# Gathers that convert on the way in, and rests between them

## The chip, the cores and the metric

The kernel runs on one core of one Trainium2 chip. The core has a matrix engine (TensorE, PE), a vector engine (VectorE, DVE), a scalar engine (ScalarE, ACT), a general engine (GpSimd, POOL) and a sync engine (SyncE, SP) that issues transfers. Sixteen DMA engines move data between the chip's main memory and the core's own memory. The metric is the device time of one launch in microseconds (us). Before the change it was 438.41 us, the median of three runs (437.76 to 445.43).

## The reference

```python
B, S, N, D = (16, 4096, 2048, 512)
gathered = x[b_idx, indices, :].copy()      # x float32 [B, S, D]; indices sorted, int64 [B, N]
cs = np.cumsum(gathered, axis=1)            # running sum over the N gathered rows of each batch
return np.matmul(cs, w).astype(np.float32)  # w float32 [D, D]; result [B, N, D]
```

For each of 16 batches, 2048 rows of 512 numbers are picked out of 4096, summed up as they come, and each running sum is multiplied by one 512 by 512 matrix. 67 MB are gathered and 67 MB are written.

## The kernel before

The 16 x 2048 output rows are cut into T = 256 tiles of 128 rows, and each two tiles form a group (R = 2). One batch is NT = 16 tiles. A tile goes through six steps, each on an engine of its own:

- `gather` (line 129, Pool): an indirect DMA fetches the tile's 128 rows of x, 256 KB, into a float32 slot `g32`. There are NG = 16 tile slots. A gather into a used slot first waits until the cast of the tile that was there is done (semaphore `s_c`).
- `cast` (line 150, ScalarE): copies the slot to float16 in `g16` (16 tiles as well). `casts` (lines 116 to 124) is a list worked out beforehand of which tiles are cast at which step: up to FAR = 6 tiles ahead, mostly two tiles in one instruction of 1024 columns, and one at a time near both ends.
- `sums` (line 158, PE): four matmuls with a triangular matrix of ones. Each gives, for 128 of the 512 columns, the running sums inside the tile, already transposed, in a PSUM buffer `pa` (NA = 4).
- `carry` (line 175, DVE): adds the last column of the tile before and writes float16 to `cst`. Each carry needs the one before it. At the start of a batch it is a plain copy (line 185).
- `project` (line 202, PE): four matmuls of `cst` with the float16 matrix `w16` into a PSUM buffer `pb` (NB = 4).
- `drain` (line 219, ScalarE): copies `pb` to one of NO = 4 output buffers `ob`, four tiles each.

SyncE stores an output buffer, 1 MB, as soon as its four tiles are drained (`store`, line 224); the first and last two groups are stored in smaller pieces. ScalarE works through its steps strictly in order: at each fourth tile it waits until the output buffer's last store is done (`s_o`), then come the casts of that step, then the drain. PE's order is a list written out beforehand (lines 350 to 358): LEAD = 3 tiles of sums ahead of the projections. Inside the sums and the projections stand waits for the buffer that the next step needs, between the first and second or the second and third matmul. DVE, PE and ScalarE run the middle of the work in hardware loops (`Fori`), 16 tiles a turn; Pool's and SyncE's instructions are written out in full. Ahead of all this the indices are loaded, transposed on PE to one per partition, and written back as integers.

In an ordinary group the tiles' rows are interleaved: partition p of the group's tiles holds neighbouring rows, so that one store descriptor covers two rows. The groups in `PLAIN`, the first two and the last two, are in plain row order, so that each tile can be summed, projected and stored by itself.

Of the kernel before, what the change touches and what calls it, by code (L numbers as in the profile page):

```python
# [7 lines left out]
P = 128  # L8
FP32 = mybir.dt.float32
FP16 = mybir.dt.float16  # L10
# [23 lines left out]
def kernel(  # L34
# [7 lines left out]
    nc = tc.nc  # L42

    B, S, D = x.shape
    N = indices.shape[1]
    R = 2
# [3 lines left out]
    T = B * NT  # L50
    G = T // R
# [1 line left out]
    KI = T // P  # L53
    FIRST = 2 * R
    NG = 16
    LEAD = 3
    FAR = 6
    NH = 8
    NA = 4
    NB = 4  # L60
    NC = 4
    W = 2
    H = 1
    NO = 4
    U = NT
    V = max(U, W * R * NO)
    assert V % U == 0 and V % (W * R * NO) == 0 and T % V == 0 and U % NG == 0 and U % NA == 0 and U % (R * NC) == 0 and U % NB == 0
    assert D == 512 and N % (R * P) == 0 and T % P == 0

    x_flat = x.rearrange("b s d -> (b s) d")  # L70
# [1 line left out]
    const = ctx.enter_context(tc.tile_pool(name="const", bufs=1))  # L72
# [8 lines left out]
    ut = const.tile([P, R, Q], FP16)  # L81
    uq = const.tile([P, P], FP16)
    ident = const.tile([P, P], FP32)
    zeros = const.tile([P, D], FP16)
    spare = const.tile([P, 1], FP16)
    g32 = [const.tile([P, R, D], FP32, name=f"g32_{i}") for i in range(NG // R)]
    g16 = [const.tile([P, R, D], FP16, name=f"g16_{i}") for i in range(NH)]
    cst = [const.tile([P, DC, R, P], FP16, name=f"cst{i}") for i in range(NC)]
    ob = [const.tile([P, W, R, D], FP32, name=f"ob{i}") for i in range(NO)]
    pa = [ps.tile([P, DC, R, Q], FP32, name=f"pa{i}") for i in range(NA)]  # L90
# [11 lines left out]
    s_w = [sem(f"s_w{c}") for c in range(DC)]  # L102
    s_idx = [sem(f"s_idx{k}") for k in range(KI)]
    s_ol = sem("s_ol")
    s_g = [sem(f"s_g{i}") for i in range(NG)]
    s_o = [sem(f"s_o{i}") for i in range(NO)]
    s_a = sem("s_a")
    s_d = sem("s_d")
    s_b = sem("s_b")
    s_e = sem("s_e")  # L110

    pool, pe, dve, act, sp = (
        Lane(e) for e in (nc.gpsimd, nc.tensor, nc.vector, nc.scalar, nc.sync)
    )

    casts = []
    cast_by = []
    for u in range(T):
        far = min(FAR, 2 if u < R else 3 + (u + 4) // 8, 3 + (T - 1 - u) // 6)
        casts.append([])  # L120
        while len(cast_by) <= min(u + far, T - 1):
            n = R if far > 5 and len(cast_by) % R == 0 else 1
            casts[u].append((len(cast_by), n))
            cast_by += [cast_by[-1] + 1 if cast_by else 1] * n

    for u in range(2 * U + U, T - 2 * U):
        assert casts[u] == [(t + U, n) for t, n in casts[u - U]]

    def gather(t):
        g, r = divmod(t, R)  # L130
        if t >= NG:
            pool.need(s_c, cast_by[R * (g + 1) - NG - 1])
        if t < FIRST:
            pool.need(s_first[g], 16)
            ap = idx_first[:, t, 0:1]
        else:
            pool.need(s_prep, t // P + 1)
            ap = idxg[:, t // P, t % P : t % P + 1]
        nc.gpsimd.indirect_dma_start(  # L139
            out=g32[g % (NG // R)][:, r, :],  # L140
            out_offset=None,
            in_=x_flat,
            in_offset=bass.IndirectOffsetOnAxis(ap=ap, axis=0),
            element_offset=(t // NT) * S * D,
        ).then_inc(s_g[t % NG], 16)


    PLAIN = (0, 1, G - 2, G - 1)

    def cast(t, n, first=None):  # L150
        g, r = divmod(t, R)
        for u in range(t, t + n):
            act.need(s_g[u % NG], 16 * (u // NG + 1), first)
        nc.scalar.copy(  # L154
            out=g16[g % NH][:, r : r + n], in_=g32[g % (NG // R)][:, r : r + n]
        ).then_inc(s_c, 1)

    def sums(t, u, first=None):
        g, r = divmod(t, R)
        tiles = None if first is None else R * first  # L160
        pe.need(s_c, cast_by[t] if first is None else cast_by[2 * U + t] - 2 * U // R, first)
        pe.need(s_d, t - NA + 1, tiles)
        for c in range(DC):
            if c == 1 and u is not None:
                pe.need(s_e, u - NB + 1, tiles)
            mm = nc.tensor.matmul(  # L166
                out=pa[t % NA][:, c],
                lhsT=g16[g % NH][:, r, c * P : (c + 1) * P],
                rhs=uq[:] if first is None and g in PLAIN else ut[:],
                start=(c == 0),  # L170
                stop=(c == DC - 1),
            )
        mm.then_inc(s_a, 1)
# [28 lines left out]
    def project(u, t, first=None):  # L202
        g, j = divmod(u, R)
        tiles = None if first is None else R * first
        pe.need(s_e, u - NB + 1, tiles)
        pe.need(s_d, u + 1 if first is None and g in PLAIN else R * (g + 1), tiles)
        for c in range(DC):
            if c == 2 and t is not None:
                pe.need(s_d, t - NA + 1, tiles)
            mm = nc.tensor.matmul(  # L210
                out=pb[u % NB][:],
                lhsT=cst[g % NC][:, c, j, :],
                rhs=w16[:, c, :],
                start=(c == 0),
                stop=(c == DC - 1),
            )
        mm.then_inc(s_b, 1)
# [6 lines left out]
    def store(g, n):  # L224
        b, h = divmod(g, GB)
        rows = out[b, h * R * P : (h + n) * R * P, :]
        src = ob[g // W % NO]
        if g in (0, G - 1):
            for j in range(R):
                sp.need(s_e, R * g + j + 1)  # L230
                nc.sync.dma_start(
                    out=rows[j * P : (j + 1) * P, :], in_=src[:, g % W, j]
                ).then_inc(s_ol if g else (s_o[0], s_of)[j >= H], 16)
            return
        sp.need(s_e, R * (g + n))
        order = "(g j p) d -> p g j d" if g in PLAIN else "(g p j) d -> p g j d"
        rows = rows.rearrange(order, p=P, j=R)
        src = src[:, g % W : g % W + n]
        if n < W:
            done = s_ol if g >= W else (s_o[0], s_of)[R + g > H]  # L240
            nc.sync.dma_start(out=rows, in_=src).then_inc(done, 16)
            return
        for i in range(H):
            part = slice(i * P // H, (i + 1) * P // H)
            nc.sync.dma_start(out=rows[part], in_=src[part]).then_inc(s_o[g // W % NO], 16)
# [23 lines left out]
    for g in range(G - W, G):  # L269
        store(g, 1)  # L270
    for i in range(G // W - NO, G // W - 1):
        sp.need(s_o[i % NO], 16 * H * (i // NO + 1))
    sp.need(s_ol, 16 * (R + W - 1))


# [4 lines left out]
        out=ident[:],  # L280
        in_=ident[:],
# [7 lines left out]
        out=ut[:],  # L289
        in_=ut[:],  # L290
# [9 lines left out]
        out=uq[:],  # L300
        in_=uq[:],
# [5 lines left out]
    ).then_inc(s_ut, 1)  # L307
    for t in range(T):
        gather(t)
    nc.gpsimd.drain()  # L310


# [12 lines left out]
    for k in range(KI):  # L325
# [3 lines left out]
            out=pb[k % NB][:, :P], in_=idxf[:, k, :], identity=ident[:]  # L329
# [29 lines left out]

    head = order.index((False, 2 * U - 1)) + 1  # L360
    tail = order.index((False, T - 2 * U - 1)) + 1
    step = 2 * U
    for i in range(head + step, tail):
        assert order[i] == (order[i - step][0], order[i - step][1] + U)

    def run(i, first=None):
        is_sums, t = order[i]
        after = next((v for k, v in order[i + 1 :] if k != is_sums), None)
        if first is not None:
            t -= 2 * U  # L370
            after -= 2 * U
        if is_sums:
            sums(t, after, first)
        else:
            pe.need(s_wc, DC)
            project(t, after, first)

    for i in range(head):
        run(i)
    with nc.tensor.Fori(2 * U // R, (T - 2 * U) // R, U // R) as first:  # L380
        pe.new_pass()
        for i in range(head, head + step):
            run(i, first)
# [19 lines left out]

    for u in range(2 * U):
        step(u)
    with nc.scalar.Fori(2 * U, T - 2 * U, V) as first:
        act.new_pass()
        for u in range(V):
            step(u, first)
    for u in range(T - 2 * U, T):  # L410
        step(u)
# [30 lines left out]
```

## Time and profile before

| what | value |
|---|---|
| median of three runs | 438.41 us |
| profiled execution | 440.94 us |
| its span, first to last instruction | 439.2 us |
| granted TensorE clock, mean | 0.892 |
| HBM read and written | 68.42 MB, 67.11 MB |
| longest chain: PE, issue, DVE, unknown queue | 74%, 10%, 7%, 7% |

The profile is of one execution. Busy times are given per engine; a group of instructions is one source line with one shape, with its count, its busy time in us, the mean of one in ns, and the idle time ahead of it by what ended it. A row of waits gives the waiting instruction, what it waited for, the total in us, the number of times and the longest. A row of the order in time starts with its start and its duration in us, and ends with the idle time ahead of it. "issue" is idle time without a wait that the profile shows, and "remote" stands for a queue or core that it cannot name. In the row of digits, each digit is the busy share of the DMA engines in one of 40 equal slices, in tenths. In the table by stage, x stands for how many instructions started in it, and PEclk for the granted clock.

### The profile page before, as it was taken

How to read it: one execution, taken by the hardware profiler on the slowest of the kernel's cores; microseconds unless marked ns; L12 is line 12 of the kernel's file. 1: busy time of each engine (PE TensorE's matmuls, PEld its weight loads, DVE VectorE, ACT ScalarE, POOL GpSimd, SP SyncE). 2: the span in 40 equal slices, each digit the busy share in tenths (PEclk: the TensorE clock that was granted, in tenths of full speed). 3: DMA queues.
4: the chain of work that ended last, by engine and by line, in shares of the span. 5: the costliest groups of instructions: out<-in, count | busy, mean ns of one | idle time of the engine just before them, and what ended most of it. 6: DMA issues, size and time to landing. Idle time of an engine off the chain costs nothing.

```text
span 439.2 us, 6408 instructions
## 1 busy us (share of the span) xinstructions
PE 329.8 (75%) x2066; PEld 171.5 (39%) x2066; DVE 178.4 (41%) x263; ACT 263.6 (60%) x407; POOL 243.7 (55%) x266
## 2 busy tenths in 40 slices
PE   6518687777877786679787697768777697876995
PEld 2203343343434343335344353434334343443552
DVE  2104343444344444345344344344345353543552
ACT  4216566556665665576656575566576666665794
POOL 6764557565655566556565465565555665655300
PEclk9756989798989899988899698996989969998898
DMA  7864979799888999989898899988989999999966
GB/s 225 256 212 156 347 273 344 252 336 364 285 318 304 333 351 328 350 294 339 316 353 295 310 336 335 359 318 273 366 310 328 331 337 328 300 330 349 331 242 241
DMA packets 39884, 135.68 MB, mean 309 GB/s; under 512 B 5825, under 2 KB 6081, under 8 KB 39873
## 3 DMA queue, kind: packets, MB, share of 16 engines
q0 software_dynamic: 20480, 67.13, 47.9%
q1 hardware_dynamic: 18832, 67.90, 38.9%
q10 hardware_dynamic: 560, 0.53, 0.4%
q8 instruction: 5, 0.08, 0.1%
q14 instruction: 7, 0.05, 0.0%
HBM read 68.42 MB, written 67.11 MB: 309 GB/s over the span
## 4 chain that ended last, share of the span: by engine, by line
PE 74%; issue 10%; DVE 7%; another core or an unknown queue 7%; ACT 1%; DVEq 0%; ACTq 0%; SPq 0%
PE pb L210 55%; PE pa L166 18%; DVE cst L198 7%; PE pb L316 1%; DVE cst L185 0%; ACT ob L222 0%; ACT g L154 0%; PE pb L328 0%; DVEq L26 0%; DVE zeros L320 0%; DVEq L437 0%; ACTq L26 0%; SPq L93 0%
## 5 line engine op out<-in xcount | busy, mean ns | idle before, releaser
L210 PE MATMUL pb<-w,cst 128*128 128x512 f16 x1024 | 293.1, 414 | 84.7 <-DVE cst L198 60.1
L139 POOL DMA_INDIRECT g<-in_x_dram,idxg x252 | 238.2, 945 | 165.1 <-ACT g L154 97.6
L198 DVE TENSOR_TENSOR cst<-pa,cst 128x512 f16<-128x512 f32 x240 | 166.1, 692 | 231.3 <-PE pa L166 162.2
L222 ACT COPY ob<-pb 128x512 f32<-128x512 f32 x256 | 146.2, 591 | 164.6 <-PE pb L210 108.1
L210 PEld LDWEIGHTS pb<-w,cst 128*128 128x128 f16 x1024 | 94.3, 104 | 164.9 <-DVE cst L198 65.8
L154 ACT CAST g<-g 128x1024 f16<-128x1024 f32 (+1 forms) x147 | 138.4, 945 | 0.3 <-issue 0.2
L166 PE MATMUL pa<-ut,g 128*128 128x128 f16 x992 | 103.9, 230 | 16.0 <-issue 12.8
L166 PEld LDWEIGHTS pa<-ut,g 128*128 128x128 f16 x992 | 81.5, 104 | 87.7 <-issue 33.8
L185 DVE CAST cst<-pa 128x512 f16<-128x512 f32 x16 | 11.0, 686 | 16.2 <-PE pa L166 12.6
L316 PE MATMUL pb<-zeros 128*128 128x512 f16 x16 | 5.9, 538 | 1.5 <-DVE zeros L320 1.5
L139 POOL DMA_INDIRECT g<-in_x_dram,idx_first x4 | 4.0, 994 | 1.6 <-issue 0.9
L166 PE MATMUL pa<-uq,g 128*128 128x128 f16 x32 | 3.1, 219 | 1.9 <-issue 1.8
L166 PEld LDWEIGHTS pa<-uq,g 128*128 128x128 f16 x32 | 2.2, 97 | 4.2 <-issue 3.1
L316 PEld LDWEIGHTS pb<-zeros 128*128 128x128 f16 x16 | 2.1, 135 | 4.2 <-issue 2.2
L392 ACT CAST w<-w 128x512 f16<-128x512 f32 x2 | 1.1, 616 | 3.4 <-DMA w<-in_w_dram 3.4
L389 ACT ACT_TABLE_LOAD x1 | 1.3, 1283 | 2.5 <-issue 2.5
L323 DVE CAST idxf<-idx 128x128 f32<-128x128 uint32 x2 | 0.5, 227 | 3.8 <-DMA idx<-in_indices_dram 3.8
L337 DVE CAST w<-w 128x512 f16<-128x512 f32 x2 | 0.8, 422 | 1.6 <-DMA w<-in_w_dram 1.6
L328 PE MATMUL pb<-ident,idxf 128*128 128x128 f32 x2 | 0.9, 447 | 0.0
L328 PEld LDWEIGHTS pb<-ident,idxf 128*128 128x128 f32 x2 | 0.4, 206 | 0.9 <-issue 0.9
L320 DVE MEMSET zeros<- 128x256 uint32 x1 | 0.3, 272 | 1.1 <-SPq L93 1.1
L334 DVE CAST idxg<-pb 128x128 uint32<-128x128 f32 x2 | 0.6, 292 | 0.3 <-PE pb L328 0.2
(11 smaller groups left out, 2.1 us busy)
## 6 DMA issues: line engine op xcount, KB each, us to landing
out_dram<-ob SPq DMA_DIRECT2D x62, 1024.0 KB
g<-in_x_dram,idxg POOLq DMA_INDIRECT x252
out_dram<-ob SPq DMA_DIRECT2D x4, 256.0 KB, 2.8
out_dram<-ob SPq DMA_DIRECT2D x2, 512.0 KB, 3.4
w<-in_w_dram ACTq DMA_DIRECT2D x2, 256.0 KB, 3.3
w<-in_w_dram SPq DMA_DIRECT2D x2, 256.0 KB
idx<-in_indices_dram SPq DMA_DIRECT2D x2, 128.0 KB, 2.6
g<-in_x_dram,idx_first POOLq DMA_INDIRECT x4
```

The source lines that it names most:

```text
L139: nc.gpsimd.indirect_dma_start(out=g32[g % (NG // R)][:, r, :], out_offset=None, in_=x_flat, in_offset=bass.IndirectOffsetOnAxis(ap=ap, ax ...
L154: nc.scalar.copy(out=g16[g % NH][:, r : r + n], in_=g32[g % (NG // R)][:, r : r + n]).then_inc(s_c, 1)
L166: mm = nc.tensor.matmul(out=pa[t % NA][:, c], lhsT=g16[g % NH][:, r, c * P : (c + 1) * P], rhs=uq[:] if first is None and g in PLAIN else ...
L185: nc.vector.tensor_copy(out=dst, in_=src).then_inc(s_d, 1)
L198: nc.vector.tensor_tensor(out=dst, in0=src, in1=last, op=mybir.AluOpType.add).then_inc(s_d, 1)
L210: mm = nc.tensor.matmul(out=pb[u % NB][:], lhsT=cst[g % NC][:, c, j, :], rhs=w16[:, c, :], start=(c == 0), stop=(c == DC - 1),)
L222: nc.scalar.copy(out=ob[g // W % NO][:, g % W, j], in_=pb[u % NB][:]).then_inc(s_e, 1)
L316: nc.tensor.matmul(out=pb[NB - 1][:], lhsT=zeros[:, :P], rhs=zeros[:], start=True, stop=True)
L328: nc.tensor.transpose(out=pb[k % NB][:, :P], in_=idxf[:, k, :], identity=ident[:]).then_inc(s_pt, 1)
L337: nc.vector.tensor_copy(out=w16[:, c, :], in_=w32[:, c, :]).then_inc(s_wc, 1)
L389: nc.scalar.copy(out=spare[:], in_=zeros[:, :1])
L392: nc.scalar.copy(out=w16[:, c, :], in_=w32[:, c, :]).then_inc(s_wc, 1)
```

## The change

The gather writes float16. Its target is `g16` itself, now the only set of gather slots, 16 tiles; the conversion takes place in the DMA. `g32`, `cast`, `casts` and FAR are gone, so ScalarE only drains. A gather into a used slot waits for PE's sums of the tile that was there (`s_a`), once for each pair of tiles. Sums wait for the gather itself (`s_g`, now 32 semaphores for 16 slots, which suits the longer loop of PE). LEAD is 4. After each four gathers Pool sets one row of 512 float16 numbers per partition of an otherwise unused tile `rest` to zero. PE's loop holds 32 tiles a turn. In its loop the tile numbers are absolute. The stores keep their pieces and their rows; the code that names their semaphores is shorter, and H, which was 1, is gone. The first and last two groups stay in row order.

```diff
     NG = 16
-    LEAD = 3
-    FAR = 6
-    NH = 8
+    NS = 32
+    FREE = 2
+    LEAD = 4
...
     U = NT
-    V = max(U, W * R * NO)
+    V = NS
...
-    g32 = [const.tile([P, R, D], FP32, name=f"g32_{i}") for i in range(NG // R)]
-    g16 = [const.tile([P, R, D], FP16, name=f"g16_{i}") for i in range(NH)]
+    rest = const.tile([P, T // NB, D], FP16)
+    g16 = [const.tile([P, R, D], FP16, name=f"g16_{i}") for i in range(NG // R)]
...
-    s_g = [sem(f"s_g{i}") for i in range(NG)]
+    s_g = [sem(f"s_g{i}") for i in range(NS)]
...
     def gather(t):
         g, r = divmod(t, R)
-        if t >= NG:
-            pool.need(s_c, cast_by[R * (g + 1) - NG - 1])
+        if t % FREE == 0:
+            pool.need(s_a, t + FREE - NG)
...
         nc.gpsimd.indirect_dma_start(
-            out=g32[g % (NG // R)][:, r, :],
+            out=g16[g % (NG // R)][:, r, :],
...
-        ).then_inc(s_g[t % NG], 16)
+        ).then_inc(s_g[t % NS], 16)
...
     def sums(t, u, first=None):
         g, r = divmod(t, R)
         tiles = None if first is None else R * first
-        pe.need(s_c, cast_by[t] if first is None else cast_by[2 * U + t] - 2 * U // R, first)
-        pe.need(s_d, t - NA + 1, tiles)
+        skip = 0 if first is None else 2 * U
+        pe.need(s_g[t % NS], 16 * (t // NS + 1) - skip // R, first)
+        pe.need(s_d, t - NA + 1 - skip, tiles)
...
-                lhsT=g16[g % NH][:, r, c * P : (c + 1) * P],
-                rhs=uq[:] if first is None and g in PLAIN else ut[:],
+                lhsT=g16[g % (NG // R)][:, r, c * P : (c + 1) * P],
+                rhs=uq[:] if g in PLAIN else ut[:],
...
     for t in range(T):
         gather(t)
+        if t % NB == NB - 1:
+            nc.gpsimd.memset(rest[:, t // NB, :], 0.0)
...
-    with nc.tensor.Fori(2 * U // R, (T - 2 * U) // R, U // R) as first:
+    with nc.tensor.Fori(2 * U // R, (T - 2 * U) // R, V // R) as first:
...
     def step(u, first=None):
-        if first is None and u == min(W * R * NO, 2 * U - 1):
-            act.need(s_of, 16 * (R + W - 1 - H))
         if u % (W * R) == 0:
-            stored = first if first is None else first * (16 * H) // (R * W * NO)
-            act.need(s_o[u // R // W % NO], 16 * H * (u // R // W // NO), stored)
-        for t, n in casts[u if first is None else 2 * U + u]:
-            cast(t if first is None else t - 2 * U, n, first)
+            if first is None and u == W * R * NO:
+                act.need(s_of, 16 * (R + W - 2))
+            act.need(s_o[u // R // W % NO], 16 * (u // R // W // NO), first)
         drain(u, first)
```

More of the change, by code (lines that the diff above doesn't have):

```diff
@@ L62 @@
     W = 2
-    H = 1
     NO = 4
     U = NT
-    V = max(U, W * R * NO)
-    assert V % U == 0 and V % (W * R * NO) == 0 and T % V == 0 and U % NG == 0 and U % NA == 0 and U % (R * NC) == 0 and U % NB == 0
+    V = NS
+    assert V % NS == 0 and NS % NG == 0 and FREE == R and NS == 16 * R and 2 * U % NS == 0 and (T - 4 * U) % V == 0 and U % (W * R * NO) == 0 and U % NA == 0 and U % (R * NC) == 0 and U % NB == 0
     assert D == 512 and N % (R * P) == 0 and T % P == 0
@@ L114 @@
     )
[L116 to L127, printed above, removed]
     def gather(t):
         g, r = divmod(t, R)
-        if t >= NG:
-            pool.need(s_c, cast_by[R * (g + 1) - NG - 1])
+        if t % FREE == 0:
+            pool.need(s_a, t + FREE - NG)
         if t < FIRST:
@@ L144, in gather @@
             element_offset=(t // NT) * S * D,
-        ).then_inc(s_g[t % NG], 16)
+        ).then_inc(s_g[t % NS], 16)
     PLAIN = (0, 1, G - 2, G - 1)
[L150 to L156, printed above, removed]
     def sums(t, u, first=None):
@@ L160, in sums @@
         tiles = None if first is None else R * first
-        pe.need(s_c, cast_by[t] if first is None else cast_by[2 * U + t] - 2 * U // R, first)
-        pe.need(s_d, t - NA + 1, tiles)
+        skip = 0 if first is None else 2 * U
+        pe.need(s_g[t % NS], 16 * (t // NS + 1) - skip // R, first)
+        pe.need(s_d, t - NA + 1 - skip, tiles)
         for c in range(DC):
             if c == 1 and u is not None:
-                pe.need(s_e, u - NB + 1, tiles)
+                pe.need(s_e, u - NB + 1 - skip, tiles)
             mm = nc.tensor.matmul(
                 out=pa[t % NA][:, c],
-                lhsT=g16[g % NH][:, r, c * P : (c + 1) * P],
-                rhs=uq[:] if first is None and g in PLAIN else ut[:],
+                lhsT=g16[g % (NG // R)][:, r, c * P : (c + 1) * P],
+                rhs=uq[:] if g in PLAIN else ut[:],
                 start=(c == 0),
@@ L204, in project @@
         tiles = None if first is None else R * first
-        pe.need(s_e, u - NB + 1, tiles)
-        pe.need(s_d, u + 1 if first is None and g in PLAIN else R * (g + 1), tiles)
+        skip = 0 if first is None else 2 * U
+        pe.need(s_e, u - NB + 1 - skip, tiles)
+        pe.need(s_d, (u + 1 if g in PLAIN else R * (g + 1)) - skip, tiles)
         for c in range(DC):
             if c == 2 and t is not None:
-                pe.need(s_d, t - NA + 1, tiles)
+                pe.need(s_d, t - NA + 1 - skip, tiles)
             mm = nc.tensor.matmul(
@@ L230, in store @@
                 sp.need(s_e, R * g + j + 1)
+                done = s_ol if g else (s_o[0], s_of)[j]
                 nc.sync.dma_start(
                     out=rows[j * P : (j + 1) * P, :], in_=src[:, g % W, j]
-                ).then_inc(s_ol if g else (s_o[0], s_of)[j >= H], 16)
+                ).then_inc(done, 16)
             return
         sp.need(s_e, R * (g + n))
[L236 to L245, printed above, removed]
+        done = {1: s_of, G - W: s_ol}.get(g, s_o[g // W % NO])
+        nc.sync.dma_start(
+            out=rows.rearrange(
+                "(g j p) d -> p g j d" if g in PLAIN else "(g p j) d -> p g j d", p=P, j=R
+            ),
+            in_=src[:, g % W : g % W + n],
+        ).then_inc(done, 16)
     with nc.allow_non_contiguous_dma(reason="a few indices, one per partition"):
@@ L271 @@
     for i in range(G // W - NO, G // W - 1):
-        sp.need(s_o[i % NO], 16 * H * (i // NO + 1))
+        sp.need(s_o[i % NO], 16 * (i // NO + 1))
     sp.need(s_ol, 16 * (R + W - 1))
@@ L361 @@
     tail = order.index((False, T - 2 * U - 1)) + 1
-    step = 2 * U
+    step = 2 * V
     for i in range(head + step, tail):
-        assert order[i] == (order[i - step][0], order[i - step][1] + U)
+        assert order[i] == (order[i - step][0], order[i - step][1] + V)
     def run(i, first=None):
@@ L368, in run @@
         after = next((v for k, v in order[i + 1 :] if k != is_sums), None)
-        if first is not None:
-            t -= 2 * U
-            after -= 2 * U
         if is_sums:
@@ L405 @@
         step(u)
-    with nc.scalar.Fori(2 * U, T - 2 * U, V) as first:
+    with nc.scalar.Fori(2 * U, T - 2 * U, U) as first:
         act.new_pass()
-        for u in range(V):
+        for u in range(U):
             step(u, first)
```

## The prediction

> **What bounds the kernel now.** I read the page's busy times and DMA lines first, then the busy time by stage, then who waits for whom, then single groups and the order in time.
>
> ```profile
> span 439.2 us, 6408 instructions
> PE 329.8 (75%) x2066; PEld 171.5 (39%) x2066; DVE 178.4 (41%) x263; ACT 263.6 (60%) x407; POOL 243.7 (55%) x266
> ...
> DMA  7864979799888999989898899988989999999966
> ...
> q0 software_dynamic: 20480, 67.13, 47.9%
> q1 hardware_dynamic: 18832, 67.90, 38.9%
> ```
>
> No engine is full; the 16 DMA engines are, in most slices. Queue 0 holds the gathers, queue 1 the stores with a few small loads. Their shares of the span are 0.479 x 439.2 = 210.4 us and 0.389 x 439.2 = 170.8 us, over 256 tiles 0.822 us for a gather and 0.667 us for a tile's store: 1.489 us a tile, 381 us in all. The stages:
>
> ```profile
> core 0: us, PE busy (x) PEld busy (x) DVE busy (x) ACT busy (x) POOL busy (x), PEclk, DMA share, GB/s
> 0.00:40.00 40.00, 19.15 (x80) 8.21 (x81) 8.00 (x16) 11.84 (x21) 25.72 (x36) 0.71 0.70 216
> 40.00:400.00 360.00, 280.02 (x1795) 147.28 (x1793) 153.15 (x223) 224.78 (x341) 211.59 (x225) 0.91 0.91 322
> 400.00:440.00 40.00, 30.61 (x192) 15.96 (x192) 17.29 (x25) 27.01 (x46) 6.34 (x7) 0.87 0.73 277
> ```
>
> The middle stage takes 82% of the span. Its POOL column counts 225 gathers in 360 us, 1.60 us each, with the DMA engines busy for 0.91 of the time: DMA work sets the pace, and 9% of it is lost. The waits say who holds whom:
>
> ```profile
> DVE cst L198 <- PE pa L166: 162.2, 118, 5.7
> ACT ob L222 <- PE pb L210: 108.1, 81, 3.5
> POOL g L139 <- ACT g L154: 97.6, 42, 5.1
> POOL g L139 <- issue: 68.4, 213, 1.2
> ...
> ACT ob L222 <- remote: 46.2, 15, 7.6
> ```
>
> Pool's only long wait is for a ScalarE cast that frees a float32 slot (97.6 us in 42 waits). The cast stands in ScalarE's order behind waits for output buffers and for projections, so a late store also holds gathers back. PE is not the limit when nothing holds it. After the last gathers DVE's steps come every 1.09 us, which is PE's own pace per tile, 278 us for 256 tiles:
>
> ```profile
> 415.09 0.69 DVE L198 TENSOR_TENSOR cst<-pa,cst 128x512 f16<-128x512 f32 x1 [0.39 <-PE pa L166]
> 416.18 0.69 DVE L198 TENSOR_TENSOR cst<-pa,cst 128x512 f16<-128x512 f32 x1 [0.40 <-PE pa L166]
> ...
> 432.03 0.69 DVE L198 TENSOR_TENSOR cst<-pa,cst 128x512 f16<-128x512 f32 x1 [0.40 <-PE pa L166]
> ```
>
> **The casts.** They go from ScalarE:
>
> ```profile
> L222 ACT COPY ob<-pb 128x512 f32<-128x512 f32 x256 | 146.2, 591 | 164.6 <-PE pb L210 108.1 <-remote 46.2 <-issue 10.1
> ...
> L154 ACT CAST g<-g 128x1024 f16<-128x1024 f32 x109 | 115.2, 1057 | 0.0
> ...
> L154 ACT CAST g<-g 128x512 f16<-128x512 f32 x38 | 23.4, 623 | 0.3 <-issue 0.2
> ```
>
> 109 x 1.057 + 38 x 0.623 = 139 us of ScalarE work disappear, leaving 146 us of copies. ScalarE is not what ends the steady stage, so its own time is worth nothing directly; with PE at 278 us as cover it would have to pass 278 us before it cost anything. What counts is that sums no longer wait for a cast and that a gather no longer waits behind a ScalarE queue held by a store.
>
> The next two parts rest on these rows, of Pool's and ScalarE's order in time and of groups on Pool:
>
> ```profile
> 3.17 1.14 POOL L139 DMA_INDIRECT g<-in_x_dram,idx_first  x1 [0.69 <-DMA idx_first<-in_indices_dram]
> ...
> 8.79 1.94 ACT L154 CAST g<-g 128x512 f16<-128x512 f32 x3 [0.21 <-issue]
> ...
> 203.24 0.94 POOL L139 DMA_INDIRECT g<-in_x_dram,idxg  x1 [1.31 <-ACT g L154]
> 204.49 0.94 POOL L139 DMA_INDIRECT g<-in_x_dram,idxg  x1 [0.30 <-issue]
> 205.73 0.95 POOL L139 DMA_INDIRECT g<-in_x_dram,idxg  x1 [0.30 <-issue]
> ```
>
> ```profile
> L139 POOL DMA_INDIRECT g<-in_x_dram,idxg x252 | 238.2, 945 | 165.1 <-ACT g L154 97.6 <-issue 67.4
> ...
> L277 POOL MEMSET ut<- 128x128 f16 x1 | 0.2, 204 | 0.0
> ...
> L426 POOL MEMSET const-bfloat16-1.0<- 128x1 bf16 x1 | 0.1, 110 | 0.0
> ```
>
> **The slots.** There are still 16, but a slot is now free when the sums of its tile are done, not when it has been cast. A pair of gathers t, t+1 waits for the sums of tile t-15. Queued behind that wait on Pool are the memset and all later gathers; who waits for those is PE. The order lets sums run up to four tiles ahead of projections (three before), so gathers run some 19 tiles ahead of the copies. At 1.5 us a tile that covers 28 us, against a first gather that was issued at 3.17 us and used by 8.79 us, 5.6 us later. I cost the smaller distance at nothing; without that cover it would cost part of 5.6 us for each pair.
>
> **The memsets.** A gather costs Pool 0.945 + 0.30 = 1.245 us. The memsets of 128 and of 1 elements differ by 94 ns, 0.74 ns an element, so 512 elements take about 0.49 us. Four gathers and a memset take 4 x 1.245 + 0.49 = 5.47 us, or 5.77 us if the memset has an issue gap of 0.30 us too: 1.37 to 1.44 us a tile, 1.41 taken. 64 memsets are 31 to 51 us on Pool. While the pace is 1.5 or 1.6 us a tile they lie inside Pool's waits (97.6 us now) and cost nothing. Where DMA is faster than 1.41 us a tile, they set the pace.
>
> **The converting gathers.** This is the open price: no row shows a DMA that converts. It still reads 256 KB a tile but writes 128 KB. On Pool I take the plain 0.945 us, since the number of rows is the same. On the DMA engines the bounds are half the present gather, 0.411 us, if only written bytes count, and upwards no row gives an end: twice, 1.64 us, would be a conversion at half the rate. A store that moves the same 256 KB takes 0.667 us, and I take that as what a transfer that reads 256 KB needs. The gather's excess over it, 0.155 us, I halve with the bytes written: 0.745 us. That is near both measured rows; the ends stay for the range.
>
> One rule stands against this choice. The Trainium skill, "DMA: Bandwidth & Descriptors", section "Anatomy of one DMA — SWDGE (gpsimd) path", fits a software-generated DMA as 2.0 us plus its bytes over 436 GB/s; by that the moving part would fall from 0.60 to 0.30 us if bytes written count, and the present 0.822 us lies above its figure for the plain gather. It does not say which side of a converting DMA counts. It would put the time at the second case below, not at my sum.
>
> **The start.** DVE stands still for 12.64 us until 32.88 us:
>
> ```profile
> 19.55 0.69 DVE L198 TENSOR_TENSOR cst<-pa,cst 128x512 f16<-128x512 f32 x1 [5.71 <-PE pa L166]
> 32.88 0.69 DVE L198 TENSOR_TENSOR cst<-pa,cst 128x512 f16<-128x512 f32 x1 [12.64 <-remote]
> ```
>
> The wait is for something the profile cannot name, while gathers are issued without a pause. In the first 40 us the DMA share is 0.70, so 12 us of DMA time are unused. With slots freed by PE the first burst ends some tiles earlier and has rests in it; I count at most a few us for this, inside the pace below.
>
> **The rest.** PE's loop body covers 32 tiles in place of 16, absolute tile numbers replace shifted ones, stores go out in the same rows, sizes and order. The first and last groups keep their row order. I cost these at nothing: the same matmuls and store issues remain. What hides a longer loop body is PE's idle time (439 - 330 us); without it a pause at each of six loop turns would count.
>
> **Sum.** DMA work per tile 0.745 + 0.667 = 1.412 us. With the casts out of the chain I let half of the lost 9% come back, a share of 0.95: 1.412 / 0.95 = 1.486 us a tile, above Pool's 1.41. The first gather is issued at 3.2 us; 255 more take 379 us: 382.2 us. When the last pair is issued the sums of tile 240 are done: 15 tiles at 1.09 us are 16.3 us, and from the last DVE step (432.03) to the end (439.2) it is 7.2 us. The span is 405.7 us. The profiled execution took 440.94 us, 1.7 us over its span and 2.5 us above the median of 438.41 us, so the median comes to **405 us**. Own range: with a gather at the store's 0.667 us Pool's 1.41 binds, 255 x 1.41 + 26.7 = 386 us; at 0.822 us and the 0.95 share 1.567 x 255 + 26.7 = 426 us.
>
> **Rivals.**
> Pool-paced: the conversion halves the engine time. Then DMA needs 0.411 + 0.667 = 1.08 us, PE 1.09 us, and Pool's 1.37 to 1.44 us set the pace; no backlog at the end, so 3.2 + 255 x 1.41 + 5.6 (landing) + 4.4 (four tiles of lead) + 7.2 = 380 us, between 370 and 390. For it: half the bytes go into SBUF, and gathers cost more per byte than stores. Against: the read side is unchanged.
> Nothing moves: the gather keeps 0.822 us, the lost 9% stays, because it comes from stores and gathers blocking each other and not from casts. 426 to 447 us, 438 in the middle. For it: DMA's 0.91 share already.
> Slower, by the DMA queue: a converting packet takes longer. It decides early: 2% over the median is a span of 448 us, (448 - 26.7) / 255 x 0.95 - 0.667 = 0.90 us a gather, 10% above now. At 25% more (1.03 us) it is 1.784 x 255 + 26.7 = 482 us; at twice, 647 us. For it: conversion is added work in a queue that is the bound. Against: nothing seen, only that the engines write less.
> Slower, by Pool: writing a converting gather's transfers takes longer than 0.945 us. It decides at 1.19 us, where 4 x 1.49 + 0.64 = 6.6 us for four tiles gives 1.65 us a tile; at 1.42 us it is about 506 us.
>
> **Chances.** Forecast 0.40, Pool-paced 0.22, nothing moves 0.16, slower by DMA 0.16, slower by Pool 0.06. About 2% is what a measurement of this kernel can tell from no change. Faster holds the first two and a small part of the third below 429.6 us, 0.65; same 0.13; slower 0.22. The range of 372 to 470 us takes in the bounds of forecast and Pool pace and the near part of the slower cases; about 0.04 lies below and 0.16 above. The forecast alone has 386 to 426 us.
>
> **What would show it.** Queue 0's share times the span over 256 gives the converting gather: 0.745 us by forecast, 0.41 Pool-paced, above 0.9 slower. Pool's group of gathers should stay near 945 ns and its memsets near 490 ns, 64 of them. Pool's long waits should be for L166, 20 to 60 us in all, and nearly none if Pool sets the pace. The middle stage should show the DMA share at 0.95 and ScalarE at 146 us. The forecast is wrong if gathers keep 0.82 us with a share of 0.91, or if PE is found waiting for gathers that land late although Pool waits for nothing.

## The result and the profile after

The changed kernel takes 404.82 us (median of 4 runs, 404.53 to 406.5), beside 440.81 us for the kernel before on the same chip: a ratio of 0.921 with an interval of 0.913 to 0.930. The forecast was 405 us. The number held; the reason given for it did not, as the experiments show.

One thing is needed to read the numbers below. The kernels of one comparison ran on one chip, but not every comparison got the same one, and the kernel before took 441 to 445 us in three of the comparisons and 350 us in two. I call these the 440 and the 350 setting. The result above and the trace of before belong to the 440 setting. The changed kernel itself was not run in the 350 setting; two kernels close to it were, with LEAD 3 and with extra work on ScalarE, and there they took 4 to 5% longer than the kernel before. Times are medians of all executions, while a ratio leaves out those more than 1.5% above the fastest of their kernel (among them one of 614.68 us of the kernel with smaller casts), so it can differ a little from the quotient of two medians.

The page of the changed kernel, with busy times, the DMA engines in 40 slices, and the two big queues:

```profile
span 402.9 us, 6104 instructions
...
DMA  7988999999999999999999999999999999999985
...
q0 software_dynamic: 36864, 33.57, 58.2%
q1 hardware_dynamic: 18832, 67.90, 43.1%
...
L125 POOL DMA_INDIRECT g<-in_x_dram,idxg x252 | 237.1, 941 | 100.6 <-issue 54.6
...
L202 ACT COPY ob<-pb 128x512 f32<-128x512 f32 x256 | 142.0, 590 | 248.3 <-PE pb L190 196.8
L289 POOL MEMSET rest<- 128x512 f16 x64 | 34.8, 543 | 0.1
```

A gather's 128 rows are now 1 KB each: 33.57 MB in place of 67.13, in more packets. By the prediction's way of counting, 0.582 x 402.9 / 256 = 0.916 us of engine time go to a gather (0.822 before) and 0.678 us to a tile's store. By this count, halving the written bytes made no gather cheaper. The busy time by stage and the waits:

```profile
core 0: us, PE busy (x) PEld busy (x) DVE busy (x) ACT busy (x) POOL busy (x), PEclk, DMA share, GB/s
40.00:320.00 280.00, 232.58 (x1513) 118.93 (x1514) 130.78 (x190) 104.19 (x189) 203.34 (x237) 0.95 1.05 263
```

```profile
DVE cst L177 <- PE pa L145: 163.3, 122, 4.3
POOL g L125 <- issue: 55.5, 200, 0.3
...
DVE cst L177 <- remote: 31.3, 22, 5.0
POOL g L125 <- PE pa L145: 23.1, 38, 1.4
PE pb L190 <- DVE cst L177: 23.0, 18, 5.9
POOL g L125 <- remote: 22.9, 17, 2.5
```

The DMA share of 1.05 is above 1, since packets of one engine can overlap in the records. Pool's long waits are now for sums (L145 and "remote", 46 us together). The projections' wait for DVE's carry is 23.0 us. The same row of the kernel before, which the prediction did not quote, was

```profile
PE pb L210 <- DVE cst L198: 60.1, 30, 7.5
```

That is 37.1 us less waiting on PE, in a span that is 36.3 us shorter. In the 440 setting this row is at 60 and 75 us in the two profiles with casts in the path, and at 22 to 39 us in the six without. The row tells the two kinds of kernel apart, but it is no price: between 22 and 39 us, and between 60 and 75 us, the time is the same.

### The profile page after: what moved, and what is told of

It reads as the page before. It is cut to its first block, busy times and chain, and to the rows that moved or that the text cites. A ratio compares the mean times of both kernels' runs of the same rounds, so it can differ in the third digit from the quotient of the medians.

```text
span 402.9 us, 6104 instructions
## 1 busy us (share of the span) xinstructions
PE 323.7 (80%) x2066; PEld 164.3 (41%) x2066; DVE 178.9 (44%) x263; ACT 144.6 (36%) x260; POOL 277.2 (69%) x330
## 3 DMA queue, kind: packets, MB, share of 16 engines
q0 software_dynamic: 36864, 33.57, 58.2%
## 4 chain that ended last, share of the span: by engine, by line
PE 76%; issue 12%; DVE 4%; another core or an unknown queue 2%; DMA 2%; POOL 2%; ACT 1%; DVEq 0%; SPq 0%
PE pb L190 58%; PE pa L145 18%; DVE cst L177 4%; POOL g L125 1%; DMA g<-in_x_dram,idxg 1%; ACT ob L202 1%; DMA idx_first<-in_indices_dram 0%; POOL rest L289 0%; DVEq L26 0%; SPq L411 0%; SPq L92 0%
## 5 line engine op out<-in xcount | busy, mean ns | idle before, releaser
L190 PE MATMUL pb<-w,cst 128*128 128x512 f16 x1024 | 284.0, 401 | 46.0 <-DVE cst L177 23.0
L202 ACT COPY ob<-pb 128x512 f32<-128x512 f32 x256 | 142.0, 590 | 248.3 <-PE pb L190 196.8
L190 PEld LDWEIGHTS pb<-w,cst 128*128 128x128 f16 x1024 | 89.7, 102 | 126.4 <-issue 44.0
L145 PE MATMUL pa<-ut,g 128*128 128x128 f16 x992 | 106.7, 226 | 25.1 <-issue 23.7
L145 PEld LDWEIGHTS pa<-ut,g 128*128 128x128 f16 x992 | 78.0, 102 | 97.9 <-issue 45.9
L289 POOL MEMSET rest<- 128x512 f16 x64 | 34.8, 543 | 0.1
L145 PE MATMUL pa<-uq,g 128*128 128x128 f16 x32 | 3.1, 219 | 0.8 <-DMA g<-in_x_dram,idx_first 0.8
L145 PEld LDWEIGHTS pa<-uq,g 128*128 128x128 f16 x32 | 2.4, 97 | 2.7 <-DMA g<-in_x_dram,idx_first 1.0
```

Of the source, the lines that this page charges most:

```text
L145: mm = nc.tensor.matmul(out=pa[t % NA][:, c], lhsT=g16[g % (NG // R)][:, r, c * P : (c + 1) * P], rhs=uq[:] if g in PLAIN else ut[:], star ...
L190: mm = nc.tensor.matmul(out=pb[u % NB][:], lhsT=cst[g % NC][:, c, j, :], rhs=w16[:, c, :], start=(c == 0), stop=(c == DC - 1),)
L202: nc.scalar.copy(out=ob[g // W % NO][:, g % W, j], in_=pb[u % NB][:]).then_inc(s_e, 1)
L289: nc.gpsimd.memset(rest[:, t // NB, :], 0.0)
```

## The experiments

By the prediction's account the DMA engines set the pace, and casts in the path from gather to sums made them idle. The other accounts put the gain into the conversion itself or into ScalarE's freed time, or hold that the memsets take back a part of it.

**Without the memsets, and with memsets of twice the size** (440 setting; before 442.86 us).

```diff
 for t in range(T):
     gather(t)
-    if t % NB == NB - 1:
-        nc.gpsimd.memset(rest[:, t // NB, :], 0.0)
```

> The changed kernel without its 64 memsets, nothing else. Theory A (the DMA engines set the pace and the memsets lie inside Pool's waits, as predicted): 400 to 409 us against 404.8, and Pool's waits for slots grow from 46 to about 80 us. Theory B (the memsets matter, because they keep gathers from crowding out stores and PE): 415 to 430 us. Theory C (Pool sets the pace with 1.38 us a tile): 375 to 390 us.

Measured: 405.79 us, ratio 0.918 (0.910 to 0.927).

```diff
-    rest = const.tile([P, T // NB, D], FP16)
+    rest = const.tile([P, T // NB, 2 * D], FP16)
```

> The changed kernel with memsets of twice the width, 1024 numbers. By its groups Pool then needs 4 x 1.241 + about 1.0 = 6.0 us for four tiles, 1.50 us a tile, just above the present 1.47. Theory A: Pool becomes the bound, 3.2 + 255 x 1.50 + 24 = 410 us, 406 to 414. Theory B: below 404 us if more rest helps more. Theory C: 410 us as well, with Pool's waits gone.

Measured: 404.34 us, 0.918 (0.909 to 0.927). The group of memsets and Pool's waits with doubled memsets:

```profile
L289 POOL MEMSET rest<- 128x1024 f16 x64 | 62.0, 969 | 0.0
```

```profile
POOL g L125 <- remote: 7.3, 19, 0.4
POOL g L125 <- PE pa L145: 7.3, 31, 0.4
```

Pool's waits for sums and "remote" are 73 us without memsets, 46 us with them and 15 us with doubled ones. The memsets lie wholly inside these waits, as predicted. The 406 to 414 us expected for doubled memsets were too high: 1.50 us a tile had been estimated for Pool, and with 15 us of waits left it was not yet the bound at 1.47.

**The kernel before with the memsets alone** (same comparison).

```diff
 for t in range(T):
     gather(t)
+    if t % NB == NB - 1:
+        nc.gpsimd.memset(rest[:, t // NB, :], 0.0)
```

> The kernel before with the same 64 memsets on Pool, no other change. Theory A: no change, 436 to 443 us, since the memsets lie inside the 97.6 us that Pool waits. Theory B (the rests are worth something by themselves): 415 to 430 us.

Measured: 440.47 us, 0.996 (0.991 to 1.001). Two of its waits:

```profile
PE pb L211 <- DVE cst L199: 75.5, 34, 7.7
POOL g L140 <- ACT g L155: 66.9, 33, 3.0
```

Pool's wait for casts fell from 97.6 to 66.9 us and the time did not move. So of that wait, on which the prediction built, at least these 31 us were slack.

**The changed kernel without the conversion** (same comparison). The slots are float32 again and gathers are plain; sums read the upper 16 bits of each number as float16, so that no cast is needed (what they add up is then not x).

```diff
-    g16 = [const.tile([P, R, D], FP16, name=f"g16_{i}") for i in range(NG // R)]
+    g16 = [const.tile([P, R, D], FP32, name=f"g16_{i}") for i in range(NG // R)]
...
-                lhsT=g16[g % (NG // R)][:, r, c * P : (c + 1) * P],
+                lhsT=g16[g % (NG // R)][:, r, c * P : (c + 1) * P].bitcast(FP16)[:, 1::2],
```

> The changed kernel with plain float32 gathers into 16 float32 slots and no cast anywhere: the sums read the upper halves of the numbers in place as if they were float16, so the values summed are others than the reference's. It keeps the short chain (no ScalarE cast, slots freed by PE, memsets) and drops only the conversion. Theory A (the gain came from taking the cast out of the chain): 400 to 412 us. Theory D (the gain came from half the bytes written): 430 to 440 us. Queue 0 should cost 0.82 us a tile again instead of 0.916.

Measured: 404.89 us, 0.918 (0.910 to 0.926). Its gather queue and its middle stage:

```profile
q0 software_dynamic: 20480, 67.13, 50.7%
```

```profile
40.00:320.00 280.00, 228.26 (x1521) 116.25 (x1520) 130.92 (x191) 104.57 (x189) 204.28 (x236) 0.97 0.97 352
```

Twice the bytes land in the slots, the gather takes 0.507 x 403.2 / 256 = 0.80 us in place of 0.916, the share is 0.97 in place of 1.05, and the time is the same to 0.1 us. In this setting the conversion is worth nothing in either direction, and a price that moves by 13% without moving the time is not the bound.

**ScalarE's work without the dependence.** The changed kernel gets the old casts back on ScalarE, in order and size, from a constant tile into scratch.

```diff
+        for t, n in casts[u if first is None else 2 * U + u]:
+            g, r = divmod(t, R)
+            nc.scalar.copy(out=scr[g % 8][:, r : r + n], in_=w32[:, r : r + n, :])
         drain(u, first)
```

It came to the 350 setting first, where it can't decide, and then to the 440 setting.

> The changed kernel, and ScalarE does the old casts' copies again by the old list, at the old places, but from a constant tile into a scratch tile that nobody reads: 139 us more work on ScalarE, no wait added. Theory A1 (as predicted: ScalarE's own time is worth nothing, the waits on the cast were the loss): 402 to 408 us. Theory A2 (the loss was ScalarE's time: with 1.03 us a tile it cannot catch up after a stall): 425 to 442 us.

Measured, beside before at 349.89 us: 365.32 us, 1.045 (1.043 to 1.048).

> The changed kernel with ScalarE given the kernel before's casts again, in the same order and sizes, but from a constant tile into scratch, so that nothing waits for them except what stands behind them on ScalarE. If before is near 441 us: theory one, that the gain came from taking the cast out of the path from gather to sums and from sums' freeing of slots, gives 402 to 408 us; theory two, that it came from ScalarE's 139 us of work, which delayed the copies and with them PE, gives 425 to 442 us. If before is near 350 us: Pool paces, ScalarE has 266 us of 360, and both theories give 361 to 367 us, nothing to tell apart; it then serves as the changed kernel's time on this chip beside the one without memsets.

Measured, beside before at 444.74 us: 406.89 us, 0.916 (0.910 to 0.923). On the page and in the waits of this run:

```profile
PE 320.4 (79%) x2066; PEld 163.3 (40%) x2066; DVE 178.8 (44%) x263; ACT 260.7 (64%) x407; POOL 277.2 (68%) x330
```

```profile
PE pb L201 <- DVE cst L188: 24.2, 20, 6.1
```

ScalarE is as busy as in the kernel before (260.7 us beside 263.6) and PE's wait for the carry stays at 24 us. The work was never the cost. What remains of the change is the cast's place between gather and sums, with the slots that the cast set free, and LEAD 4 in place of 3. PE's longer loop costs or brings nothing that the records show: at all 12 turns before and all 6 after, PE's next instruction starts within 0.2 us of the turn, while a matmul is still running.

**LEAD 3, half the stores, and smaller casts in the kernel before.** Their expectations are for the 440 setting, but they came to the 350 one (before 349.89 us). So they do not decide between the theories that they name, and show something else.

```diff
-    LEAD = 4
+    LEAD = 3
```

> The changed kernel with LEAD = 3 as before, in place of 4. Theory A: 402 to 408 us, the lead costs and brings nothing. A rival (part of the gain is that sums run one tile further ahead, which frees slots earlier): 410 to 425 us.

Measured: 364.76 us, 1.044 (1.042 to 1.046).

```diff
 def store(g, n):
...
     done = {1: s_of, G - W: s_ol}.get(g, s_o[g // W % NO])
+    n = 1
+    rows = out[b, h * R * P : (h + n) * R * P, :]
     nc.sync.dma_start(
```

With that each store of two groups writes one, and nearly half of the rows are never written.

> The changed kernel with the second half of each 1 MB store left out (those rows are not written): 0.33 us less DMA work a tile, everything else as it is. Theory A (DMA is the bound of the changed kernel): it falls until Pool's 1.38 us a tile binds, 3.2 + 255 x 1.38 + 17 = 372 us, 368 to 380. Rival P (the matrix engine's results set the pace, whatever the DMA engines do): 398 to 405 us.

Measured: 361.18 us, 1.033 (1.031 to 1.035).

```diff
-            out=g16[g % NH][:, r : r + n], in_=g32[g % (NG // R)][:, r : r + n]
+            out=g16[g % NH][:, r : r + n, :P], in_=g32[g % (NG // R)][:, r : r + n, :P]
...
-                lhsT=g16[g % NH][:, r, c * P : (c + 1) * P],
+                lhsT=g16[g % NH][:, r, :P],
```

> The kernel before, in which each cast copies only the first 128 of a tile's 512 columns, and the four matmuls of the sums all read these; three quarters of the cast are left out, all waits stay. ScalarE's casts fall from 139 to about 55 us. Theory A1 (the waits are the loss): 432 to 442 us. Theory A2 (ScalarE's time is the loss): 404 to 415 us.

Measured: 349.97 us, 1.000 (0.999 to 1.002). Once more in a second comparison of that setting (before 349.86 us):

> The kernel before with its casts in place, but each casts only a quarter of its columns, and all four matmuls of a tile's sums use that quarter. ScalarE's work falls by some 70 us; sums and slots still wait for a cast in ScalarE's order, behind copies. If before is near 441 us: theory one, that the place of the cast in the path costs the time, gives 432 to 442 us; theory two, that ScalarE's work costs it, gives 404 to 415 us. If before is near 350 us: Pool paces, and both give 347 to 351 us, as on such a chip already.

Measured: 350.14 us, 1.001 (0.999 to 1.002). Its Pool waits show what limits this form there:

```profile
POOL g L139 <- issue: 72.2, 237, 0.3
POOL g L139 <- ACT g L154: 5.5, 18, 0.3
```

Pool issues a gather every 1.25 us without rest. With the memsets, in the LEAD 3 kernel, the order of time on Pool is

```profile
201.91 0.54 POOL L289 MEMSET rest<- 128x512 f16 x1
202.61 0.95 POOL L125 DMA_INDIRECT g<-in_x_dram,idxg  x1 [0.17 <-PE pa L145]
203.87 0.94 POOL L125 DMA_INDIRECT g<-in_x_dram,idxg  x1 [0.30 <-issue]
205.11 0.94 POOL L125 DMA_INDIRECT g<-in_x_dram,idxg  x1 [0.30 <-issue]
206.35 0.94 POOL L125 DMA_INDIRECT g<-in_x_dram,idxg  x1 [0.30 <-issue]
207.29 0.54 POOL L289 MEMSET rest<- 128x512 f16 x1
```

207.29 - 201.91 = 5.38 us for four tiles, 1.345 us a tile, against 1.25. Here the memsets have no cover. And the queues and the middle stage, of LEAD 3 and then of half the stores:

```profile
q0 software_dynamic: 36864, 33.57, 60.5%
q1 hardware_dynamic: 18832, 67.90, 47.3%
```

```profile
40.00:320.00 280.00, 239.80 (x1665) 122.57 (x1664) 143.85 (x208) 121.93 (x208) 223.83 (x261) 1.00 1.12 292
```

```profile
q0 software_dynamic: 36864, 33.57, 69.8%
q1 hardware_dynamic: 10896, 35.40, 26.4%
```

```profile
40.00:320.00 280.00, 239.87 (x1665) 120.50 (x1664) 143.85 (x209) 121.88 (x208) 223.84 (x261) 1.00 0.99 195
```

The same 36,864 gather packets take 0.605 x 363.0 / 256 = 0.858 us a tile in one and 0.698 x 359.4 / 256 = 0.980 us in the other, where there is less other traffic. (LEAD differs between the two, but LEAD 4 with the dummy casts gives 0.602 x 363.7 / 256 = 0.855 us.) With nearly half the stored bytes gone the share still stands at 0.99. Packet times stretched to fill the room that there was; the share does not give a price. Both kernels issue their gathers at Pool's pace, 208 tiles in 280 us.

**Without memsets, twice more.**

> The changed kernel without its 64 memsets. Two chips have shown two paces of the kernel before: about 441 us where the DMA engines are short, about 350 us where Pool is; which one this is shows in the time of the kernel before in the same comparison. If that is near 350 us: Pool sets the pace, the memsets cost their own time there (64 x 0.54 = 35 us less 14 us for gaps that differ), and without them a gather costs Pool 0.942 + 0.30 = 1.245 us; 3.2 + 255 x 1.247 + 17 to 20 us of tail gives a span of 338 to 341 us and a time of 338 to 345 us, 2 to 3% faster than before. The rival, that the memsets lie in waits there too and something else made the changed kernel slower: 360 to 367 us. If before is near 441 us: the saturated DMA engines set the pace with and without memsets, 404 to 408 us.

Measured in the 440 setting: 405.22 us beside 444.74 us, 0.913 (0.907 to 0.919).

> The changed kernel without its 64 memsets, once more on whichever chip comes. If the kernel before takes near 350 us in the same comparison, Pool sets the pace: 3.2 + 255 x 1.247 + 17 to 20 us gives a span of 338 to 341 us and a time of 338 to 345 us, faster than before by 2 to 3%; the rival, that the memsets are not what made the changed kernel slower there, gives 360 to 367 us. If before is near 441 us, the DMA engines set the pace: 404 to 408 us.

Measured in the 350 setting: 354.91 us beside 349.86 us, 1.013 (1.012 to 1.015). Here I had expected 338 to 345 us. Of the expected terms, the pace is 1.269 us (last gather issued at 326.75 us) in place of 1.247, and from then to the end of the span at 353.9 us it is 27.2 us in place of 17 to 20; the kernel with the smaller casts needs 26.0 us there too, so the tail had been too short for both. Set beside the two kernels with memsets in the other comparison, 10 us of the 15 us loss are gone without them, and 5 us stay. Most of these 5 us are pace, 1.269 us beside 1.251 us with the smaller casts, and Pool shows what it waits for:

```profile
POOL g L125 <- PE pa L145: 18.2, 41, 1.8
```

These are waits for sums to free a slot, beside 5.5 us for casts in the other kernel. The rows that bear on why sums are late are the landing times of gathers (last column, median us from issue to landing), here

```profile
g<-in_x_dram,idxg POOLq DMA_INDIRECT x252, 14.9
```

and with plain gathers, in the smaller-cast kernel of the same comparison,

```profile
g<-in_x_dram,idxg POOLq DMA_INDIRECT x252, 10.4
```

The packets say the same: a converting gather moves one row per packet, median 98 ns, and a plain one two rows in 159 ns. A reading that fits is that in the 350 setting the gather queue is near its limit, and that the converting form reaches it first. That this makes the last 5 us is argued; a plain gather without a cast was not run there. Of the kernels run in both settings, none was faster than the kernel before in both.

## What sets the pace in the 440 setting

After all casts were out of the path, everything gave 404 to 407 us: with and without memsets, with and without conversion, with ScalarE idle or busy. Something common to these kernels sets 1.474 us a tile. Whether data is late shows in what PE waits for. In the changed kernel, 440 setting, the only wait of the sums' matmuls for a gather is the first one:

```profile
PE pa L145 <- DMA g<-in_x_dram,idx_first: 0.8, 1, 0.8
```

In the LEAD 3 kernel, 350 setting, they wait for gathers all along:

```profile
PE pa L145 <- DMA g<-in_x_dram,idxg: 50.0, 69, 2.3
```

The packet records agree. Counted in order of their ends, the packets of a gather in the 440 setting are done about 5 us after its issue, and the tile then lies in its slot for 12.6 us until its sums start; in the kernel before it lies 18.7 us until its cast and 22 us until its sums. In the LEAD 3 kernel it lies 1.7 us. So in the 440 setting neither kernel waited for gathers in the middle of the work. Nor did they wait for stores: the last packet of a store is done 5 to 6 us after the copy that released it, 8.6 us at most, and its buffer is needed again only after 12 more tiles.

Late instead is what comes out of PE. DVE starts its carry 0.04 us after the recorded end of a tile's last sums matmul when all is well. In the changed kernel's first 40 us it looks like this in the order of time:

```profile
19.74 0.69 DVE L177 TENSOR_TENSOR cst<-pa,cst 128x512 f16<-128x512 f32 x1 [1.44 <-PE pa L145]
23.25 0.69 DVE L177 TENSOR_TENSOR cst<-pa,cst 128x512 f16<-128x512 f32 x1 [2.83 <-PE pa L145]
27.49 0.69 DVE L177 TENSOR_TENSOR cst<-pa,cst 128x512 f16<-128x512 f32 x1 [3.54 <-PE pa L145]
33.13 0.69 DVE L177 TENSOR_TENSOR cst<-pa,cst 128x512 f16<-128x512 f32 x1 [4.95 <-remote]
```

The sums that the last of these waited for had ended by the records at 26.3 us. I summed over all tiles the time between the moment when, by the records, both the sums were finished and DVE was free, and DVE's start, leaving out delays up to 0.15 us. It is 173 us in the kernel before, 189 us in the changed one, 188 us without conversion, 180 us without memsets, 185 us with the dummy casts; and 0.0 us in the LEAD 3 kernel and in the one without memsets of the 350 setting. DVE is not what is late: in the changed kernel the recorded change of the semaphore comes within 0.12 us before its start in 135 of the 136 late cases, and ScalarE's copies are late by 211 us in the same way (0.0 us with LEAD 3). PE itself also stands idle where the profile shows no wait,

```profile
PE pa L145 <- issue: 23.7, 33, 2.9
PE pb L190 <- issue: 22.3, 20, 2.7
```

which the LEAD 3 kernel has in no row. The ends of matmuls are modelled in these records, so it may be that PE itself runs slower than they say, or that its signals arrive late; the records cannot tell the two apart.

The delay is spread evenly, 16 to 21 us in each 40 us up to 360 us, and it stops with the gathers: soon after the last one the carries come every 1.09 us again, as in the 350 setting. So the gathers, or what goes on beside them, may be what makes PE late in this setting. It does not follow the bytes that they write, since 263 and 352 GB/s (with and without conversion) give 189 and 188 us. Fewer stores or fewer gathers were not run in this setting, so this rival stays open.

This also gives a reading of what the casts cost. A late projection holds a copy on ScalarE, and in the kernel before the casts of later tiles stand behind that copy, so one late result of PE delays the sums that PE could have done meanwhile. From ScalarE's order in time, kernel before:

```profile
209.72 0.58 ACT L222 COPY ob<-pb 128x512 f32<-128x512 f32 x1 [2.41 <-PE pb L210]
211.92 0.58 ACT L222 COPY ob<-pb 128x512 f32<-128x512 f32 x1 [1.62 <-remote]
212.41 1.05 ACT L154 CAST g<-g 128x1024 f16<-128x1024 f32 x1
```

The cast at 212.41 us works on two tiles that had landed by 194.7 us and stands behind two late copies. Casting from a constant in the same places costs nothing (0.916), which fits. The runs show that neither ScalarE's work nor the conversion nor the memsets make the gain. They do not separate the cast's place from LEAD 4, because LEAD 3 was measured in the 350 setting alone, where it differs little (364.76 us beside 365.32 us of the kernel with LEAD 4 and dummy casts).

## Why the prediction was right in its number and wrong in its reason

- **What bounds the kernel.** "DMA work sets the pace, and 9% of it is lost" failed. It was read from a DMA share of 0.91 and never tested against what waits for the transfers. Gathers lay finished for 22 us before use, and in the 350 setting, with nearly half the stored bytes gone, the share still read 0.99. What goes with the pace in this setting is PE's late results, from a cause that stays open.
- **The price of a converting gather.** Forecast 0.745 us, measured 0.916 us, and by the prediction's own point of decision, 0.90 us, the kernel should have become slower. It became 8% faster, because such a figure is no price. The share was forecast at 0.95 and measured at 1.05. The two misses cancelled: 1.412 / 0.95 = 1.486 us a tile forecast, 1.594 / 1.05 = 1.52 us by the same division, 1.474 us measured between the first gather and the last.
- **A page's rule on it.** The Trainium skill, "DMA: Bandwidth & Descriptors", section "Anatomy of one DMA — SWDGE (gpsimd) path", has bytes over a rate; with written bytes it would have halved the moving part. The traces show no such fall: in the two kernels that differ in the conversion alone, a gather's packets are done 5.0 us after its issue in both, and the share gives 0.916 us with it and 0.80 us without.
- **The casts.** That ScalarE's "own time is worth nothing directly" held: 0.916 with ScalarE at 260.7 us, 0.913 without memsets and with ScalarE at 143.2 us in the same comparison, intervals overlapping. That "a gather no longer waits behind a ScalarE queue" was worth nothing that shows, by the kernel before with memsets and by the 18.7 us that gathers lay landed before their casts. Late stores, which the prediction put at the head of that queue, were not found. That sums no longer wait for a cast is what stays, together with LEAD.
- **The slots.** 16 were enough in this setting: 17.6 us lie between a gather's issue and its sums, of which some 12.6 us are spare.
- **The memsets.** 543 ns (forecast 490), 34.8 us, inside Pool's waits. The condition that the prediction named for their cost, a pace below 1.41 us, is what the 350 setting gives: 1.345 us a tile on Pool, and, for the two kernels with memsets that ran there, slower than before. That is the Pool-paced rival as a mechanism, at 365 us beside its 380 us.
- **Pool's gathers.** 941 ns, forecast 945. Waits for L145 and unnamed ones 46 us, forecast 20 to 60.
- **The start.** The 12.64 us stall of DVE, taken for something like a few us to win, was one of PE's late results. The longest such stall is 5.0 us after the change, and PE waits up to 13.1 us for a carry in the first run without memsets; the time is the same.
- **The sum.** First gather at 3.20 us, last at 379.0 us, 23.9 us to the end, span 402.9 us; forecast 3.2, 382.2, 23.5 and 405.7. Each term is within 2%, from a pace that was right by accident.
- **The rival that it gets slower by the DMA queue** had its mechanism (a converting packet does take longer per row, 98 ns beside 79.5) and not its effect, since the queue was not the bound.

## What to carry to other kernels

A DMA share near 1 does not show that transfers are the bound: look at how long the data lies landed before it is used, and at what the consumer waits for. In an engine that works strictly in order, keep work that others need soon from standing behind work that can be late. A cover such as "in Pool's waits" holds only where these waits exist; the same memsets cost nothing at a pace of 1.47 us a tile and some 10 us where Pool sets the pace (from kernels of two comparisons). Converting gathers with memsets won 8% in one setting, and in their two variants lost 4 to 5% in the other, so a change is only known to be faster in the settings in which it was run.

## What was not expected of the hardware

The same kernel took 440 us and 350 us in different comparisons and stayed near it within each (437.7 to 448.85 and 349.04 to 350.87 us over 13 runs each). In the 440 setting PE's results reach DVE late by up to 5 us and more while gathers run, and in the profiles of the 350 setting by 0.5 us at most. The granted clock differs, 0.95 and 1.00 in the middle stages of the changed kernel and of LEAD 3, but with doubled memsets it is 0.99 there and 0.995 over the whole profiled execution, which was no faster (404.23 us). In the 350 setting, an execution of the kernel with smaller casts at a mean of 0.852 was no slower (349.22 us). So the recorded clock is not the reason. The cause is open, and so is whether it belongs to a chip or to its condition at the time: the expectations speak of two chips, but the record has the chip number 0 for a comparison of each setting, within ten minutes, and does not tell whether that was the same chip. The Trainium skill, "TensorE: Matmul & The Clock Gate", section "What's actually happening", says that the clock gate passes either half or all of the pulses; the traces agree, with stretches of 0.5 and 1.0 and nothing between. No run here shows a slower clock that would explain 1.474 us in place of 1.09 us a tile.
